# Fifteen instead of thirteen column blocks in the first projections, and their weight loads in program order

## The chip, the cores and the metric

The kernel runs on one core of one Trainium2 chip. A core has a matrix engine (TensorE, PE in the profile), a vector engine (DVE), a scalar engine for activations and casts (ACT), GpSimd (POOL) and a synchronisation engine (SP), whose queue here starts nearly all transfers from memory. Each engine works through its own list of instructions in order and waits on semaphores for the others. The metric is the device time of one execution in microseconds (us); of several executions the median is taken.

## What is computed

One layer of a hybrid decoder, 256 tokens of width 2048, everything in float32:

```
mod = silu(c) @ w_ada + b_ada                       # six rows of 2048: sh1, sc1, gt1, sh2, sc2, gt2
h = rmsnorm(x, g_mix) * (1 + sc1) + sh1
z = h @ w_in
(mq, mk, mv, mo, mi, mf, dq, dk, dv, sq, sk, sv, gm, gd, gs) = split_cols(z, IN_SIZES)
out_m = mlstm(mq, mk, mv, mi, mf, mo)
out_d = differential_attention(dq, dk, dv)
out_s = stick_breaking_attention(sq, sk, sv)
merged = (sigmoid(gm) * (out_m @ w_branch[0])
          + sigmoid(gd) * (out_d @ w_branch[1])
          + sigmoid(gs) * (out_s @ w_branch[2]))    # gs, the third gate: 2048 columns, in four blocks of 512
x = x + gt1 * (merged @ w_out)
h = rmsnorm(x, g_ffn) * (1 + sc2) + sh2
hid = h @ w_up
x = x + gt2 * ((silu(causal_dwconv(hid[:, :5632])) * hid[:, 5632:]) @ w_down)
```

What the change touches is the projection `z = h @ w_in` and, in it, the columns of `gs`.

## The kernel before, in words

**Matrix products in three passes.** Weights and activations are float32. `weights()` (L330) loads 4 k-tiles (4 x 128 rows) of a column block of up to 512 columns, 1 MB, in one transfer on SP's queue (L337) into one of three buffers `raw`; ACT casts two k-tiles at a time into a rounded part `hi` (L342), DVE subtracts to get the rest `lo` (L344), and `gemm()` (L350) sums three products: hi by both parts of the activations, lo by the rounded part. So a block of 512 columns over all 16 k-tiles is 96 matmuls of 512 columns: per k-tile and token half, three of them. There are four buffers each for `hi` and `lo`. Blocks of only 2 k-tiles use a smaller buffer, `raw2`. Results gather in banks of PSUM: three called `gp` and four called `mx` (the function `bank`), which short work uses.

**The start.** `h` is not there at once: its scale and shift come from `silu(c) @ w_ada`, a product that DVE does by multiply-add (`ada_mac`, L217) while 4096 columns of `w_ada` arrive. It is made in pieces of 2 to 4 k-tiles: k-tiles 0 and 1 first, 2 and 3 next (`ada_first`), then 4 to 7, 8 to 11 and 12 to 15 (`ada_quad`, L272). Each finished piece lets `make_h` (L458) produce those k-tiles of `h`. Meanwhile the first projections run on the k-tiles that exist. The list `first` (L508 to L516) holds 13 column blocks: 0 to 3 are sq and sk, 4 and 5 are sv, 6 to 12 are 440 columns wide and hold mi, mf, dq, dk and dv. `visit()` (L560) goes over a range of blocks up to a given k-tile and sets a rate; `partial()` (L521) does one block from the k-tile where it stopped. Between visits the partial sums of a block lie in the destination tile. They are copied out by ACT (L549), copied back into PSUM (L538) before the next visit, or added by DVE (L551); blocks 0 and 1 keep banks of their own.

**Side work.** After each group of 4 k-tiles `tick()` (L209) takes steps from two lists: `ada` (the pieces of w_ada) and `side` (everything else that can lie beside matmuls). `rates` says how many steps a tick takes. When the k-tiles wanted aren't there, `partial` takes steps until they are.

**Order of transfers.** A load in `weights()` carries `issue_after(state["load"].ins)`, that is, it's placed behind the load before it in SP's queue, only the first time (`started`, L335). Later ones may be placed earlier by the scheduler that lays out each engine's list. The steps of `ada` always carry it (L262, L278, L292).

**Behind the first projections.** A last loop (L892 to L895) brings the 13 blocks to k-tile 16; at block 5 it appends `stick()`, stick-breaking attention, to the side list. `stick` goes through four pairs of heads. Each pair works in the tile `ez` in slot 9 (a slot is one of the large tiles, `slot(i, name)`): scores, log terms, sums along the row through `puA` and `puB` (L615 to L620), subtraction (L621, L622), exponential (L623), masks (L626, L627), then the product with sv into `po` (L632, L634), which is split into `osh` and `osl` (L636). Behind the loop the gate blocks 0 and 1 of `gs` go into `mg0` (slot 8), the side list is emptied, `mg1` is allotted in slot 9, where `ez` was, `diff()` is appended (its first step squares dq into `dsq`, L645), and gate blocks 2 and 3 go through a sigmoid on ACT (L851) into `mg1`.

`late_vectors()` (L138) loads small vectors on POOL's queue into `rows2`, a tile in slot 3, where the input x lay until it was transposed at the start.

Of the kernel before, what the change touches and what calls it, by code (L numbers as in the profile page):

```python
# [12 lines left out]
AF = mybir.ActivationFunctionType  # L13
# [4 lines left out]
P = 128  # L18
# [21 lines left out]
def kernel(  # L40
# [97 lines left out]
    def late_vectors():  # L138
        rows = slot(3, "rows2")
        rowsB, rowsC = rows[0:27, 0:P], rows[0:64, P:2 * P]  # L140
        rowsD = rows[0:NF, 2 * P:5 * P].rearrange("k (j p) -> k j p", j=3)
        def ld(*args):
# [11 lines left out]
        ld(bif, b_gate_if.rearrange("o (g h) -> h (o g)", h=MH))  # L154
        lamv = rows[0:1, 640:896].rearrange("o (v d) -> o v d", v=4)
        for i, lv in enumerate((lam_q1, lam_k1, lam_q2, lam_k2)):
# [11 lines left out]

        lp = rows[0:1, 896:1024].rearrange("o (v d) -> o v d", v=2)
        V.tensor_tensor(lp, lamv[:, 0::2, :], lamv[:, 1::2, :], ALU.mult)  # L170
# [21 lines left out]
    ada = deque()  # L192
    state = {"ada": 0.0, "side": 0.0, "split": None, "load": None, "hold": None, "h": 0, "started": False}

# [135 lines left out]
    def weights(rows, nk, n, hold=None):  # L330
        if nk == 2:
            raw = adap.tile([P, 2, 512], F32, tag="ada", name="raw2")
        else:
            raw = rawp.tile([P, 4, 512], F32, tag="raw", name="raw")
        with tc.issue_after(state["load"].ins) if not state["started"] else nullcontext():  # L335
            state["started"] = True
            state["load"] = nc.sync.dma_start(raw[:, :nk, :n], rows.rearrange("(k p) f -> p k f", p=P))  # L337
        his, los = [], []
        for k0 in range(0, nk, 2):
            hi = hip.tile([P, 2, 512], F32R, tag="hi", name="hi")  # L340
            lo = lop.tile([P, 2, 512], F32R, tag="lo", name="lo")
            A.copy(hi[:, :, :n], raw[:, k0:k0 + 2, :n])  # L342
            with tc.issue_after(hold.ins) if hold else nullcontext():
                state["split"] = V.tensor_tensor(lo[:, :, :n], raw[:, k0:k0 + 2, :n], hi[:, :, :n].bitcast(F32),  # L344
                                                 ALU.subtract)
            his.append(hi)
            los.append(lo)
        return his, los
# [166 lines left out]
    for i in range(7):  # L515
        first.append(("T", C_IF + 440 * i, 440, dest_D(i), 1.0))  # L516

    def shaped(src, dst):
        return src.rearrange("p (a b) -> p a b", a=dst.shape[1]) if len(dst.shape) == 3 else src

    def partial(ci, kt0, kt1):  # L521
# [21 lines left out]
        for b in range(2):  # L543
            for cs, d in dest(b):
# [3 lines left out]
                elif put or kt0 == 0:  # L548
                    A.copy(d, shaped(acc[b][:, cs], d))  # L549
                else:  # L550
                    V.scalar_tensor_tensor(d, shaped(acc[b][:, cs], d), scale, d, ALU.mult, ALU.add)  # L551
        tick()

# [3 lines left out]
    ada.extend(ada_quad(k0, quads[:, (i % 2) * 1024:(i % 2 + 1) * 1024]) for i, k0 in enumerate((4, 8, 12)))  # L557
    done = [0] * 13

# [5 lines left out]

    visit(range(0, 9), 2, 0.72)
    visit(range(9, 13), 4, 2.1)
    visit(range(0, 9), 4, 1.1)
    side.append(late_vectors())
    rates["side"] = 0.4  # L570
    visit(range(0, 10), 8, 1.72)
    visit(range(10, 13), 12, 1.36)
    visit(range(0, 7), 12, 1.36)
    drain(ada)
    drain(side)


# [313 lines left out]
    rates["side"] = 2.4  # L891
    for ci in range(13):  # L892
        partial(ci, done[ci], 16)
        if ci == 5:
            side.append(stick())  # L895


    rates["side"] = 2.0
    rates["ada"] = 0.9
    mg.append(slot(8, "mg0"))  # L900
    for ch in range(2):
        gates(C_GS, ch, mg_of(ch))
    drain(side)
# [213 lines left out]
```

## Time and profile before

| what | value |
|---|---|
| median of 3 runs | 1791.58 us (1788.38 to 1792.2) |
| time of the profiled execution | 1787.35 us |
| span of the profiled execution, first to last instruction | 1785.6 us |
| mean granted TensorE clock | 0.999 |
| read from memory, written | 419.68 MB, 2.10 MB |
| mean transfer rate over the span | 237 GB/s |

Times in the views are in microseconds from the first instruction of the profiled execution. Busy time of PE is the sum of stretches in which some matmul is recorded as running; a matmul's record is longer than its share of a steady stream (389 ns for 512 columns), because matmuls are pipelined and overlap. So a short wait hides in the overlap and shows in the distance of the starts rather than as idle time. In the view of windows, a row is a stretch: its length, then busy time (and count) of PE, of PE's weight loads, DVE, ACT and POOL, the granted clock, the busy share of the DMA engines, and GB/s. In a timeline row stand start, length, engine, line, operation, and in brackets how long the engine was idle ahead of it and on what it waited.

### The profile page before, as it was taken

The numbers are of one execution on the slowest core, as the hardware profiler recorded it, in microseconds if no ns is written. First come the engines' busy times: TensorE is split into PE (matmuls) and PEld (weight loads), VectorE is DVE, ScalarE is ACT, GpSimd is POOL, SyncE is SP. The second block draws the span as 40 slices with busy tenths as digits, with TensorE's granted clock in tenths as the row PEclk, the third lists the DMA queues.
The fourth block names the chain that finished last, engine by engine and source line by source line (L and its number), as shares of the span: only waits on it lengthen the run. The fifth ranks groups of instructions, "written<-read, shape, count | busy, mean of one in ns | idle before, by whom it ended". The sixth has DMA issues, their size and how long they took to land.

```text
span 1785.6 us, 23761 instructions
## 1 busy us (share of the span) xinstructions
PE 1762.2 (99%) x9168; PEld 1512.5 (85%) x9168; DVE 1302.4 (73%) x1734; ACT 951.9 (53%) x1338; POOL 16.4 (1%) x44
## 2 busy tenths in 40 slices
PE   7899999999999999999999999999999999999998
PEld 6898999888878887888888888888888888888887
DVE  6887646878888778777996577888875556666654
ACT  6667655666565556544444555555553345555432
POOL 2000000000000000000000000000000000000000
PEclk9999999999999999999999999999999999999999
DMA  9999855776777567778896547777755555555563
GB/s 338 346 330 313 289 179 178 266 244 242 248 238 259 200 216 251 240 261 294 308 323 216 181 166 259 253 251 267 268 204 198 193 189 189 189 189 189 189 214 117
DMA packets 219731, 423.33 MB, mean 237 GB/s; under 512 B 9027, under 2 KB 31675, under 8 KB 219105
## 3 DMA queue, kind: packets, MB, share of 16 engines
q1 hardware_dynamic: 217328, 417.44, 68.8%
q0 software_dynamic: 1008, 2.23, 0.4%
q10 hardware_dynamic: 1280, 2.14, 0.3%
q8 instruction: 72, 1.18, 0.3%
q14 instruction: 43, 0.34, 0.1%
HBM read 419.68 MB, written 2.10 MB: 236 GB/s over the span
## 4 chain that ended last, share of the span: by engine, by line
PE 95%; ACT 2%; DMA 1%; DVE 1%; issue 1%; SPq 0%; ACTq 0%
PE gp L391 55%; PE acch L377 32%; PE kept L396 2%; PE gp L396 2%; DMA raw<-in_w_in_dram 1%; ACT hi L342 1%; PE psc L679 0%; PE pm L240 0%; DMA x<-in_x_dram 0%; DVE quads L224 0%; PE spin L186 0%; ACT x L444 0%; PE pr L321 0%; PE pxt L453 0%; PE ptf L739 0%
## 5 line engine op out<-in xcount | busy, mean ns | idle before, releaser
L344 DVE TENSOR_TENSOR lo<-raw,hi 128x1024 fp32r<-128x1024 f32 (+1 forms) x608 | 724.0, 1208 | 363.4 <-ACT hi L342 327.1
L342 ACT CAST hi<-raw 128x1024 fp32r<-128x1024 f32 (+1 forms) x608 | 617.6, 1039 | 552.4 <-PE gp L391 353.6
L391 PE MATMUL gp<-hi,h 128*128 128x512 f32 (+1 forms) x1600 | 411.4, 387 | 7.0 <-ACT hi L342 5.7
L377 PE MATMUL acch<-h,hi 128*128 128x512 f32 x1664 | 403.3, 392 | 0.2 <-DVE h L1032 0.2
L377 PEld LDWEIGHTS acch<-h,hi 128*128 128x128 f32 x1664 | 303.6, 188 | 58.0 <-DVE h L1032 1.1
L391 PEld LDWEIGHTS gp<-hi,h 128*128 128x128 f32 x1600 | 295.7, 188 | 60.7 <-ACT hi L342 8.8
L391 PE MATMUL gp<-lo,h 128*128 128x512 f32 (+1 forms) x800 | 227.5, 384 | 0.0
L377 PEld LDWEIGHTS acch<-h,lo 128*128 128x128 f32 x1664 | 217.8, 191 | 11.1
L377 PE MATMUL acch<-h,lo 128*128 128x256 f32 x1664 | 221.3, 283 | 0.0
L224 DVE SCALAR_TENSOR_TENSOR acc<-araw,ccol,acc 128x512 f32<-128x512 f32 x240 | 179.3, 748 | 6.0 <-DMA araw<-in_w_ada_dram 4.3
L391 PEld LDWEIGHTS gp<-lo,h 128*128 128x128 f32 x800 | 149.7, 188 | 26.2 <-DVE lo L344 0.8
L391 PE MATMUL gp<-hi,atl 128*128 128x512 f32 x352 | 137.2, 390 | 0.0
L391 PE MATMUL gp<-hi,ath 128*128 128x512 f32 x352 | 136.9, 389 | 0.0
L391 PE MATMUL gp<-lo,ath 128*128 128x512 f32 x352 | 105.9, 390 | 0.0
L391 PEld LDWEIGHTS gp<-hi,atl 128*128 128x128 f32 x352 | 66.1, 188 | 13.7
L391 PEld LDWEIGHTS gp<-hi,ath 128*128 128x128 f32 x352 | 66.1, 188 | 13.7
L391 PEld LDWEIGHTS gp<-lo,ath 128*128 128x128 f32 x352 | 66.1, 188 | 13.6
L224 DVE SCALAR_TENSOR_TENSOR quads<-raw,ccol,quads 128x1024 f32<-128x1024 f32 x45 | 57.7, 1282 | 2.8 <-DMA raw<-in_w_ada_dram 2.2
L391 PE MATMUL gp<-hi,mgl 128*128 128x512 f32 x128 | 50.4, 394 | 0.0
L391 PE MATMUL gp<-hi,mgh 128*128 128x512 f32 x128 | 50.0, 392 | 0.0
L1057 DVE SCALAR_TENSOR_TENSOR y<-gsum,cols,y 128x255 f32<-128x255 f32 (+1 forms) x88 | 41.4, 479 | 3.7 <-ACT y L1055 3.5
L391 PE MATMUL gp<-lo,mgh 128*128 128x512 f32 x128 | 38.3, 391 | 0.0
(365 smaller groups left out, 1601.2 us busy)
## 6 DMA issues: line engine op xcount, KB each, us to landing
raw<-in_w_in_dram SPq DMA_DIRECT2D x98, 1024.0 KB, 5.1
raw<-in_w_up_dram SPq DMA_DIRECT2D x88, 1024.0 KB, 5.1
araw<-in_w_ada_dram SPq DMA_DIRECT2D x128, 512.0 KB, 5.9
raw<-in_w_down_dram SPq DMA_DIRECT2D x44, 1024.0 KB, 5.1
raw<-in_w_ada_dram SPq DMA_DIRECT2D x62, 512.0 KB, 5.9
raw<-in_w_branch_dram SPq DMA_DIRECT2D x24, 1024.0 KB, 5.1
raw<-in_w_in_dram SPq DMA_DIRECT2D x25, 880.0 KB, 5.0
raw<-in_w_out_dram SPq DMA_DIRECT2D x16, 1024.0 KB, 5.0
```

What stands on the lines that cost most here:

```text
L224: state["mac"] = V.scalar_tensor_tensor(acc, raw[:, k, :], ccol[:, kt:kt + 1], acc, ALU.mult, ALU.add)
L342: A.copy(hi[:, :, :n], raw[:, k0:k0 + 2, :n])
L344: state["split"] = V.tensor_tensor(lo[:, :, :n], raw[:, k0:k0 + 2, :n], hi[:, :, :n].bitcast(F32), ALU.subtract)
L377: T.matmul(acc[t][:, 0:m], lhsT=w[k // 2][:, k % 2, sl], rhs=ah(s0 + k)[:, 0:m], start=start, stop=s0 + k == kt1 - 1 and w is (wh if flip ...
L391: T.matmul(o, lhsT=a(s0 + k)[:, sl], rhs=wk[:, :n], **kw)
L396: T.matmul(o, lhsT=wk[:, sl], rhs=a(s0 + k), **kw)
L1057: V.scalar_tensor_tensor(yf[:, sft:S], src[:, 0:S - sft], wc(2 - sft), yf[:, sft:S], ALU.mult, ALU.add)
```

## The change

Three things change together.

Gate blocks 0 and 1 of `gs` become blocks 13 and 14 of `first`. Their partial sums lie in `gsp`, a tile in slot 3, and behind their last part a sigmoid writes `mg0`; the separate loop of two gate blocks behind the first projections goes away, and `mg0` is allotted ahead of the last loop. The last loop takes 13 and 14 first. Since slot 3 is taken, `late_vectors` uses two small tiles of the pool `sidewide`.

Weight loads are kept in program order up to the end of the visits (`inorder`), not only the first.

The visits and rates are others, as the diff shows.

```diff
@@ -136,9 +136,9 @@
     nlam = const.tile([P, 1], F32, name="nlam")
 
     def late_vectors():
-        rows = slot(3, "rows2")
+        rows, rows3 = sidewide("rows2"), sidewide("rows3")
         rowsB, rowsC = rows[0:27, 0:P], rows[0:64, P:2 * P]
-        rowsD = rows[0:NF, 2 * P:5 * P].rearrange("k (j p) -> k j p", j=3)
+        rowsD = rows3[0:NF, 0:3 * P].rearrange("k (j p) -> k j p", j=3)
         def ld(*args):
             with tc.issue_after(state["load"].ins):
                 nc.gpsimd.dma_start(*args)
@@ -152,7 +152,7 @@
         ld(rowsC, w_mconv[0].rearrange("j (k p) -> (j k) p", p=P))
         ld(rowsD, w_ffconv[0].rearrange("j (k p) -> k j p", p=P))
         ld(bif, b_gate_if.rearrange("o (g h) -> h (o g)", h=MH))
-        lamv = rows[0:1, 640:896].rearrange("o (v d) -> o v d", v=4)
+        lamv = rows[0:1, 2 * P:4 * P].rearrange("o (v d) -> o v d", v=4)
         for i, lv in enumerate((lam_q1, lam_k1, lam_q2, lam_k2)):
             ld(lamv[:, i, :], lv)
         yield
@@ -166,7 +166,7 @@
         V.tensor_scalar(gsub_c, gsub_c, 1.0 - LAM_INIT, None, ALU.mult)
         V.tensor_scalar(gdq_c, gdq_c, 64.0 ** -0.5, None, ALU.mult)
 
-        lp = rows[0:1, 896:1024].rearrange("o (v d) -> o v d", v=2)
+        lp = rows3[0:1, 3 * P:4 * P].rearrange("o (v d) -> o v d", v=2)
         V.tensor_tensor(lp, lamv[:, 0::2, :], lamv[:, 1::2, :], ALU.mult)
         ls = const.tile([1, 2], F32, name="ls")
         V.tensor_reduce(ls, lp, AX.X, ALU.add)
@@ -190,7 +190,7 @@
 
     side = deque()
     ada = deque()
-    state = {"ada": 0.0, "side": 0.0, "split": None, "load": None, "hold": None, "h": 0, "started": False}
+    state = {"ada": 0.0, "side": 0.0, "split": None, "load": None, "hold": None, "h": 0, "inorder": True}
 
     def pump(queue, n):
         done = 0
@@ -332,8 +332,7 @@
             raw = adap.tile([P, 2, 512], F32, tag="ada", name="raw2")
         else:
             raw = rawp.tile([P, 4, 512], F32, tag="raw", name="raw")
-        with tc.issue_after(state["load"].ins) if not state["started"] else nullcontext():
-            state["started"] = True
+        with tc.issue_after(state["load"].ins) if state["inorder"] else nullcontext():
             state["load"] = nc.sync.dma_start(raw[:, :nk, :n], rows.rearrange("(k p) f -> p k f", p=P))
         his, los = [], []
         for k0 in range(0, nk, 2):
@@ -514,6 +513,9 @@
         first.append(("T", C_SV + ch * 512, 512, dest_T(sv, ch), 1.0))
     for i in range(7):
         first.append(("T", C_IF + 440 * i, 440, dest_D(i), 1.0))
+    gsp = slot(3, "gsp")
+    for ch in range(2):
+        first.append(("T", C_GS + ch * 512, 512, dest_T(gsp, ch), 1.0))
 
     def shaped(src, dst):
         return src.rearrange("p (a b) -> p a b", a=dst.shape[1]) if len(dst.shape) == 3 else src
@@ -549,13 +551,15 @@
                     A.copy(d, shaped(acc[b][:, cs], d))
                 else:
                     V.scalar_tensor_tensor(d, shaped(acc[b][:, cs], d), scale, d, ALU.mult, ALU.add)
+                    if ci > 12:
+                        A.activation(mg_of(ci - 13)[b], d, AF.Sigmoid)
         tick()
 
     kept = {}
     quads = slot(4, "quads")
     ada.append(ada_first(2))
     ada.extend(ada_quad(k0, quads[:, (i % 2) * 1024:(i % 2 + 1) * 1024]) for i, k0 in enumerate((4, 8, 12)))
-    done = [0] * 13
+    done = [0] * 15
 
     def visit(cis, kt1, rate):
         rates["ada"] = rate
@@ -563,16 +567,17 @@
             partial(ci, done[ci], kt1)
             done[ci] = kt1
 
-    visit(range(0, 9), 2, 0.72)
-    visit(range(9, 13), 4, 2.1)
-    visit(range(0, 9), 4, 1.1)
+    visit(range(0, 9), 2, 0.6)
+    visit(range(9, 15), 4, 1.4)
+    visit(range(0, 9), 4, 0.85)
     side.append(late_vectors())
     rates["side"] = 0.4
-    visit(range(0, 10), 8, 1.72)
-    visit(range(10, 13), 12, 1.36)
-    visit(range(0, 7), 12, 1.36)
+    visit([13, 14, *range(0, 10)], 8, 1.45)
+    visit([*range(10, 13)], 8, 1.45)
+    visit([13, 14, *range(0, 6)], 12, 1.45)
     drain(ada)
     drain(side)
+    state["inorder"] = False
 
 
     def stick():
@@ -889,17 +894,15 @@
 
     ada.append(ada_rest())
     rates["side"] = 2.4
-    for ci in range(13):
+    mg.append(slot(8, "mg0"))
+    for ci in (13, 14, *range(13)):
         partial(ci, done[ci], 16)
         if ci == 5:
             side.append(stick())
-
-
-    rates["side"] = 2.0
+            rates["ada"], rates["side"] = 0.5, 2.8
+
+
     rates["ada"] = 0.9
-    mg.append(slot(8, "mg0"))
-    for ch in range(2):
-        gates(C_GS, ch, mg_of(ch))
     drain(side)
     mg.append(slot(9, "mg1"))
     side.append(diff())
```

No matmul is added or taken away. On SP's list, this is what stands where the first visit ends. `raw_586<-in_w_in` is the load of block 8 for k-tiles 0 and 1; a load of 4x440 is one of blocks 9 to 12 for k-tiles 0 to 3; `raw_793`, `raw_827` and `raw_866` are loads of blocks 0, 1 and 2 for k-tiles 2 and 3, which belong to the third visit; 2x512 of w_ada are the two halves of a step of `ada_quad`. Before:

```order
L337 DMA raw_586<-in_w_in_dram 128x2x440
L337 DMA raw<-in_w_in_dram 128x4x440
L337 DMA raw_793<-in_w_in_dram 128x2x512
L337 DMA raw_827<-in_w_in_dram 128x2x512
L279 DMA raw_651<-in_w_ada_dram 128x2x512 x2
L337 DMA raw<-in_w_in_dram 128x4x440
L337 DMA raw_866<-in_w_in_dram 128x2x512
L279 DMA raw_698<-in_w_ada_dram 128x2x512 x2
L337 DMA raw<-in_w_in_dram 128x4x440
L279 DMA raw_743<-in_w_ada_dram 128x2x512 x2
L337 DMA raw<-in_w_in_dram 128x4x440
```

With the change, from the same load (here `raw_567`) on; 4x512 are blocks 13 and 14, and `raw_869` and `raw_900` are blocks 0 and 1 of the third visit:

```order
L336 DMA raw_567<-in_w_in_dram 128x2x440
L279 DMA raw_607<-in_w_ada_dram 128x2x512 x2
L336 DMA raw<-in_w_in_dram 128x4x440 x2
L279 DMA raw_694<-in_w_ada_dram 128x2x512 x2
L336 DMA raw<-in_w_in_dram 128x4x440
L279 DMA raw_739<-in_w_ada_dram 128x2x512 x2
L336 DMA raw<-in_w_in_dram 128x4x440
L336 DMA raw<-in_w_in_dram 128x4x512
L279 DMA raw_822<-in_w_ada_dram 128x2x512 x2
L336 DMA raw<-in_w_in_dram 128x4x512
L336 DMA raw_869<-in_w_in_dram 128x2x512
L336 DMA raw_900<-in_w_in_dram 128x2x512
```

The three loads of the third visit stood among those of the second; now the third visit's loads stand behind all six of the second, and steps of w_ada lie between.

On PE's list, the end of `stick`'s fourth pair of heads, from the sums `puA` to the product `po`; `gp_3531` and `gp_3532` are the banks of gate block 2. Before:

```order
L616 MATMUL puA_3242<-loA_3235,tri_97 128x512
L619 MATMUL puA_3242<-hlB_3236,ones_r_92 128x2x128
L620 MATMUL puA_3242<-hlB_3236,ones_r_92 128x2x128
L391 MATMUL gp_3531<-hi_3585,h1_138 128x512 x4
L391 MATMUL gp_3531<-lo_3586,h1_138 128x512 x2
L391 MATMUL gp_3532<-hi_3585,h1_138 128x512 x4
L391 MATMUL gp_3532<-lo_3586,h1_138 128x512 x2
L230 MATMUL pm_3613<-ident_85,acc_3229 128x128 x4
...
L391 MATMUL gp_3531<-hi_3642,h1_139 128x512 x2
L632 MATMUL po_3293<-ez_2709,sv_303 128x256
L391 MATMUL gp_3531<-hi_3642,h1_139 128x512
L634 MATMUL po_3293<-ez_2709,sv_303 128x128
```

With the change, the same place; `gp_3559` and `gp_3560`, which hold gate block 2, are full by then, and `gp_3768` and `gp_3769` are the banks of gate block 3:

```order
L390 MATMUL gp_3768<-hi_3832,h1_138 128x512 x4
L623 MATMUL puB_3387<-hlB_3342,tri_97 128x256
L621 MATMUL puA_3386<-loA_3341,tri_97 128x512
L624 MATMUL puA_3386<-hlB_3342,ones_r_92 128x2x128
L625 MATMUL puA_3386<-hlB_3342,ones_r_92 128x2x128
L390 MATMUL gp_3768<-lo_3833,h1_138 128x512 x2
L637 MATMUL po_3399<-ez_2883,sv_303 128x256
L639 MATMUL po_3399<-ez_2883,sv_303 128x128
L637 MATMUL po_3399<-ez_2883,sv_303 128x256
L639 MATMUL po_3399<-ez_2883,sv_303 128x128
L390 MATMUL gp_3769<-hi_3772,h1_138 128x512 x4
L390 MATMUL gp_3769<-lo_3773,h1_138 128x512 x2
```

Before, 26 matmuls of gate block 2 and a transpose in four parts stood between `puA` and `po`; now two matmuls do, and the first of `gp_3769` stands behind `po`. There are three `gp` banks: `gp_3769` takes the one in which `gp_3559` lay.

On ACT's list, the same place: the exponential of the fourth pair, the split of `po` (`osh`), the first step of `diff` (`dsq`) and the sigmoid of gate block 2 (`mg1`). Before:

```order
L623 ACT_TABLE_LOAD
L623 ACTIVATE ez_2709<-ez_2709 128x768
L342 CAST hi_3698<-raw_3692 128x1024
L342 CAST hi_3744<-raw_3742 128x1024
L418 CAST osh_2707<-po_3293 128x512
L645 ACTIVATE dsq_3571<-dq_304 128x2048
L342 CAST hi_3748<-raw_3742 128x1024
L851 ACT_TABLE_LOAD
L851 ACTIVATE mg1_3530<-gp_3531 128x512
```

With the change:

```order
L341 CAST hi_3832<-raw_3826 128x1024
L628 ACT_TABLE_LOAD
L628 ACTIVATE ez_2883<-ez_2883 128x768
L417 CAST osh_2881<-po_3399 128x512
L650 ACTIVATE dsq_3599<-dq_304 128x2048
L856 ACT_TABLE_LOAD
L856 ACTIVATE mg1_3558<-gp_3559 128x512
L856 ACTIVATE mg1_3558<-gp_3560 128x512
```

The two casts behind the exponential and the one behind `dsq` are gone from here, and the sigmoid still stands behind the exponential, `osh` and `dsq`. The bank of `gp_3559` comes free when this sigmoid has read it.

## The prediction

> **What bounds the kernel now.** First the busy shares and the chain of work that ended last:
>
> ```profile
> PE 1762.2 (99%) x9168; PEld 1512.5 (85%) x9168; DVE 1302.4 (73%) x1734; ACT 951.9 (53%) x1338; POOL 16.4 (1%) x44
> PE 95%; ACT 2%; DMA 1%; DVE 1%; issue 1%; SPq 0%; ACTq 0%
> 1319.67 129.21 PE gp L391 x570
> ```
>
> PE is busy for 1762.2 of 1785.6 us, and the chain lies on it for 95%. The third row is one unbroken stretch of that chain: 570 matmuls of 512 columns in 129.21 us, 0.227 us each. That is the step of a steady stream, and since the change has the same matmuls, only time in which PE waits can be gained or lost. Second view, windows of the first 500 us (length; busy time and count of PE, weight loads, DVE, ACT, POOL; clock; DMA share; GB/s):
>
> ```profile
> 26.00:45.00 19.00, 18.01 (x122) 16.02 (x120) 16.24 (x24) 8.22 (x14) 3.48 (x7) 1.00 1.08 350
> 45.00:60.00 15.00, 13.43 (x72) 12.10 (x73) 12.29 (x19) 10.41 (x22) 0.00 (x0) 1.00 1.02 369
> 60.00:75.00 15.00, 11.98 (x61) 10.52 (x60) 10.39 (x10) 6.92 (x12) 0.00 (x0) 1.00 0.90 300
> 75.00:90.00 15.00, 15.00 (x111) 14.73 (x111) 13.78 (x13) 11.10 (x18) 0.00 (x0) 1.00 1.02 369
> 90.00:110.00 20.00, 20.00 (x123) 18.07 (x122) 19.10 (x30) 18.19 (x32) 0.00 (x0) 1.00 0.90 318
> 110.00:135.00 25.00, 24.74 (x185) 23.23 (x184) 19.52 (x18) 11.29 (x16) 0.00 (x0) 1.00 0.96 330
> 135.00:160.00 25.00, 23.16 (x116) 19.84 (x115) 20.67 (x26) 20.68 (x43) 0.00 (x0) 1.00 0.91 307
> 160.00:225.00 65.00, 64.96 (x404) 61.13 (x403) 43.65 (x44) 41.20 (x67) 0.00 (x0) 1.00 0.86 296
> 300.00:400.00 100.00, 100.00 (x477) 85.97 (x476) 81.17 (x113) 64.22 (x71) 0.00 (x0) 1.00 0.73 246
> 400.00:500.00 100.00, 100.00 (x496) 80.79 (x495) 87.54 (x146) 59.20 (x115) 0.00 (x0) 1.00 0.72 247
> ```
>
> Length less PE's busy time, summed over the first eight rows, is 0.99 + 1.57 + 3.02 + 0 + 0 + 0.26 + 1.84 + 0.04 = 7.7 us of idle PE. Behind 300 us there is none. So the early stretch, to 225 us, is what there is to gain, and everything later can only be lost. The 7.7 is a low reading, because a matmul's record outlasts its step and hides the start of each wait. I therefore also took every start of PE in this stretch (the counts of the eight rows make 1194) less the start before it and less the steady step of its shape (0.227 for 512 columns, 0.200 for 440, 0.120 for 256); the first and the last of these rows are
>
> ```profile
> 26.65 0.74 PE L396 MATMUL kept<-h,hi 128*128 128x256 f32 x4 [0.41 <-ACT h L465]
> ...
> 225.01 0.39 PE L391 MATMUL gp<-lo,h 128*128 128x512 f32 x1
> ```
>
> and the sum is 13.2 us. I take 13.2 as all that the early stretch can give. What it waits on:
>
> ```profile
> PE gp L391 <- ACT hi L342: 5.7, 5, 1.6
> PE gp L391 <- ACT gp L538: 0.9, 1, 0.9
> ...
> 60.15 0.53 ACT L549 COPY dk<-gp 128x440 f32<-128x440 f32 x1 [2.37 <-PE gp L391]
> 61.15 0.53 ACT L549 COPY dk<-gp 128x440 f32<-128x440 f32 x1 [0.47 <-PE gp L391]
> 61.57 1.75 ACT L342 CAST hi<-raw 128x880 fp32r<-128x880 f32 x2
> 62.55 0.47 PE L391 MATMUL gp<-hi,h 128*128 128x440 f32 x1 [1.44 <-ACT hi L342]
> ```
>
> Nearly all of it is a wait for the cast of the next weights, in five waits of at most 1.6 us. The timeline shows two causes behind one name. ACT works in order, so at 60 to 63 us the cast at 61.57 stands behind the copies of the block before; and where ACT itself was waiting, it was for a load, in a stretch where the DMA share is 0.90 to 1.08.
>
> **Early: two more blocks and program order.** Blocks 13 and 14 bring 4 k-tiles x 6 matmuls x 2 blocks x 0.227 = 10.9 us of PE work into the second visit, at 75 us and before, work that PE does on k-tiles of h that it has, while w_ada for the next k-tiles arrives. They bring 2 x 1 MB of loads. At the 340 GB/s that the first five rows average by their lengths, 2.1 MB are 6.2 us. So PE gets 10.9 us of cover and the transfers only 6.2 us of work: about 4.7 us of transfer time comes free for w_ada. Program order adds to it: three loads of the third visit, 0.52 MB each, stood ahead of those of the second; 1.57 MB are 4.6 us by which loads that PE waits for at 45 to 70 us can come sooner. Against it stands what order cannot mend: the casts queued behind copies, such as that of 61.57. The new blocks bring more copies of that kind (12 COPY out, 8 back, and 4 additions on DVE). ACT is busy 10.41 of 15 us and DVE 12.29 of 15 in the row from 45, so they are not full, but each copy pair of 2 x 0.53 can stand ahead of a cast. Bounds for the gain: 0 if only ACT's order and the three buffers count, 13.2 if all waits go. Following the loads by hand through the new order at 340 GB/s, h for k-tiles 4 to 7 comes some 5 us sooner against PE's work than now. I take **-5**, nearer to the waits shown for the load-bound rows (45 to 75: 1.57 + 3.02 = 4.6) than to either end.
>
> **Start: POOL.**
>
> ```profile
> 22.85 0.51 POOL L144 DMA_DIRECT2D rows<-in_g_ffn_dram  x1 [19.02 <-PE pxt L453]
> 8.81 4.74 PE L186 MATMUL spin<-ones_r 128*128 128x512 f32 x14
> ```
>
> POOL's small loads waited 19.02 us for the tile that x had held. Their new tiles are free, so they can go from 4 us on, among x and the first w_ada. They are small; between 0 and the 0.5 us of one such row I take **+0.3**.
>
> **Late: the end of stick-breaking.** Here the order of instructions shows a wait that was not there. The rows of before with which I price it:
>
> ```profile
> 294.55 0.69 DVE L621 TENSOR_TENSOR ez<-ez,puA 128x512 f32<-128x512 f32 x1
> 298.41 0.42 DVE L627 TENSOR_TENSOR ez<-ez,mstrict 128x256 f32<-128x256 f32 x1
> ...
> 382.80 0.29 PE L620 MATMUL puA<-hlB,ones_r 128*128 128x256 f32 x1
> 383.14 1.28 ACT L623 ACT_TABLE_LOAD   x1
> 383.19 0.68 DVE L621 TENSOR_TENSOR ez<-ez,puA 128x512 f32<-128x512 f32 x1
> 384.43 0.85 ACT L623 ACTIVATE ez<-ez 128x768 f32<-128x768 f32 x1
> 385.66 0.42 DVE L627 TENSOR_TENSOR ez<-ez,mstrict 128x256 f32<-128x256 f32 x1
> 390.65 0.38 PE L634 MATMUL po<-ez,sv 128*128 128x128 f32 x2
> 391.07 0.59 ACT L418 CAST osh<-po 128x512 fp32r<-128x512 f32 x1 [1.35 <-PE po L634]
> 391.55 1.92 ACT L645 ACTIVATE dsq<-dq 128x2048 f32<-128x2048 f32 x1
> 395.91 1.28 ACT L851 ACT_TABLE_LOAD   x1 [1.51 <-issue]
> 397.20 0.60 ACT L851 ACTIVATE mg<-gp 128x512 f32<-128x512 f32 x1
> ```
>
> From the end of `puA` (383.1) to the end of the masks (386.08) went 2.9 us, and PE did 26 matmuls meanwhile. In the new order two matmuls stand there, 2 x 0.227 = 0.45, then `po`. So PE waits 2.9 - 0.45 = 2.45 us. Behind `po` PE's next instruction is the first matmul of `gp_3769`, and its bank is freed only by the sigmoid that reads `gp_3559`. That sigmoid writes `mg1` into slot 9, where `ez` is until `po` has read it, so it cannot go before `po`, and in ACT's list it stands behind `osh` and `dsq` as before. From the end of `po`: 391.07 - 391.03 = 0.04, `osh` to the start of `dsq` 0.48, `dsq` 1.92, table 1.28, sigmoid 0.60, and some 0.1 to PE: 4.4 us in which PE has nothing else in its list. Everything on PE stands behind it. Nothing covers it: it costs **2.45 + 4.4 = 6.9 us**. Low bound 4.4, if PE comes late to `po` for another reason and the first wait vanishes. For the upper bound, the first pair took 294.55 to 298.83, 4.3 us (to the end of the second row), where casts and splits lay between; with 4.3 in place of 2.9 and a price of the clock of 1.6 (below) it is 9.9.
>
> The row of 383.14 weighs a rule on tables: the exponential starts 0.01 us after its 1.28 us table load. The Trainium skill, "ScalarE: Activation LUTs", section "What ACT_TABLE_LOAD costs", gives a drain of about 1.38 us besides the 1.28, 2.66 for a switch. By it the last wait would be 1.38 longer and the sum 1795.2. The trace bears out the 1.28 and shows no drain at 383.14: the cast ahead of it ended 0.02 us before, so I leave it out.
>
> **The sum.** The profiled execution took 1787.35 (its span 1785.6 and 1.75 around it): 1787.35 - 5 + 0.3 + 6.9 = 1789.55. The median shown is 1791.58, 4.23 above that execution, so on its scale the time is 1789.55 + 4.23 = **1793.8**. The rest of the edits cost nothing that I can name: 15 more ACT instructions of 0.5 us lie in stretches where ACT has 4.6 of 15 us free, and all behind 600 us is unchanged.
>
> **Rivals.**
>
> *Faster: the early waits go altogether.* Transfers are what the stretch from 26 to 75 waits for (DMA share around 1), and the loads in order end that; -13.2 + 0.3 + 6.9 gives 1785.6. Against it are the copies ahead of the casts, and the 1.84 us of waits in the row from 135, behind the last visits' loads, which the change leaves. To be faster by over 0.2% (about 3.6 us, what a measurement can tell from no change) the early gain must pass 10.8. 0.15.
>
> *Slower: the early stretch does not gain, and the change does not do what it says.* The queue is full from 26 to 60 us (350 and 369 GB/s), so the same bytes and 2.1 MB more have to pass before h is complete, whatever their order; and in the row from 60 to 75, where PE idles most, the rate is 300: there it is ACT's order and three buffers that bind. Then the gain is 0, the late wait stays, 0 + 0.3 + 6.9 gives 1798.8. It decides for slower as soon as the early gain is under 3.6. 0.25.
>
> *Slower: the pause costs clock.* The granted clock is 1.00 in every row above, and the longest wait in the early stretch is 1.6 us. The 4.4 us at `gp_3769` would be much longer. If the clock falls there, the nearest price is PE's start: 14 matmuls took 4.74 us at 8.81 instead of 14 x 0.227 = 3.18, 1.6 more; 1793.8 + 1.6 = 1795.4. 0.10. The Trainium skill, "TensorE: Matmul & The Clock Gate", section "Why this matters for your kernels", says so: no PE-idle gaps over about 3 us between bursts, or the clock goes back to half. No run here shows a gap that long.
>
> **How the numbers follow.** The forecast, 1793.8, has 0.50. Its own spread, gains of 3 to 7.5 early, gives 1791.3 to 1795.8. The cases of slower hold 0.25, half of 0.10, and of the forecast the part with a gain under 3.6, some 0.07: 0.37. Faster 0.15, within 0.2% the remaining 0.48. The range takes in both ends, the faster rival at 1785.6 and the slower one at 1798.8 with something for the clock: 1785 to 1800.
>
> **What would show it.** Early: idle PE from 26 to 225 us down from 7.7 to about 3 to 5, with fewer waits for `hi`. Late: two waits of PE near the end of `stick`, one at `po` for DVE's masks of 2 to 3 us, one at the next `gp` for ACT of about 4.4, with PE's busy time in that window below its length for the first time behind 300 us. I am wrong if that second wait is absent or under 2 us, if the early idle time doesn't fall, or if the granted clock after the wait is below 1.

## The result, and the profile after

| | median | lowest to highest | runs |
|---|---|---|---|
| before | 1789.53 us | 1786.35 to 1792.77 | 14 |
| with the change | 1794.3 us | 1791.88 to 1796.72 | 14 |

The ratio is 1.0023, with a 95% interval of 1.0016 to 1.0031: the change makes the kernel slower by about 4 us (the two medians lie 4.8 apart). The profiled execution, the shortest of the 14, has a span of 1790.2 us where before had 1785.6, 4.6 more. The page of the changed kernel, its busy shares and the dearest group of matmuls:

```profile
PE 1763.7 (99%) x9168; PEld 1515.1 (85%) x9168; DVE 1305.5 (73%) x1738; ACT 965.8 (54%) x1353; POOL 16.3 (1%) x44
L390 PE MATMUL gp<-hi,h 128*128 128x512 f32 (+1 forms) x1600 | 411.0, 386 | 8.1 <-ACT mg L856 4.4
```

PE has the same 9168 matmuls. What ends most of the idle time ahead of `gp` is now the sigmoid that writes `mg`, 4.4 us, where it was the cast `hi`. The early stretch as one window, of before and then of the changed kernel:

```profile
26.00:225.00 199.00, 191.28 (x1183) 175.66 (x1182) 155.65 (x177) 128.02 (x219) 3.48 (x7) 1.00 0.93 320
```

```profile
26.00:225.00 199.00, 195.31 (x1161) 178.32 (x1161) 156.15 (x174) 135.23 (x224) 0.00 (x0) 0.99 0.93 322
```

Idle PE went from 199 - 191.28 = 7.7 to 199 - 195.31 = 3.7 us. Summed over the distances of starts, as in the prediction, the time above the steady step went from 13.2 to 8.2 (with other steps for the small shapes both are 1 to 1.5 higher, and the fall 5.3). The profiles of the runs below that leave the early stretch alone bear the fall out: idle PE in this window is 7.7 to 9.4 us in the three with the stretch of before (before, e6, e12) and 3.3 to 4.6 in the eight with that of the changed kernel (it, e1 to e3, e7 to e10). Their spread, up to 1.7 us with the same instructions, is also how far one profile can be trusted here.

The first matmul on `h` starts later with the change, at 27.73 us where the prediction shows 26.65 for before. On ACT, the third cast of weights stands ahead of the rows that make `h`; it waited for its load and began at 26.12, where before had it at 25.05:

```profile
26.12 1.05 ACT L341 CAST hi<-raw 128x1024 fp32r<-128x1024 f32 x1 [0.35 <-DMA raw<-in_w_in_dram]
27.08 1.09 ACT L464 ACTIVATE h<-xnT,b,a 128x256 fp32r<-128x256 f32 x2
27.73 1.01 PE L395 MATMUL kept<-h,hi 128*128 128x256 f32 x3 [0.83 <-ACT h L464]
```

PE's largest waits from 26 to 225 us, with the change:

```profile
PE gp L390 <- DVE h L418: 1.4, 1, 1.4
PE kept L395 <- ACT h L464: 0.8, 1, 0.8
PE gp L390 <- ACT h L417: 0.5, 1, 0.5
PE gp L390 <- ACT hi L341: 0.4, 2, 0.2
```

The waits for the cast of the next weights, 5.7 us before, are 0.4. What is left is mostly a wait for h itself. Later, where the view of before names no wait of PE from 225 to 600 us, there are now these (and one of 0.2 at `ptf`):

```profile
PE gp L390 <- ACT mg L856: 4.4, 1, 4.4
PE po L637 <- DVE ez L631: 1.8, 1, 1.8
PE gp L390 <- ACT mv L928: 1.2, 1, 1.2
```

The first two lie together. The timeline of the changed kernel there (PE and ACT, and DVE's masks):

```profile
397.33 0.63 PE L390 MATMUL gp<-lo,h 128*128 128x512 f32 x2
398.33 0.84 ACT L628 ACTIVATE ez<-ez 128x768 f32<-128x768 f32 x1 [3.94 <-DVE ez L626]
399.55 0.42 DVE L632 TENSOR_TENSOR ez<-ez,mstrict 128x256 f32<-128x256 f32 x1
399.78 0.67 PE L637 MATMUL po<-ez,sv 128*128 128x256 f32 x2 [1.82 <-DVE ez L631]
...
401.36 0.58 ACT L417 CAST osh<-po 128x512 fp32r<-128x512 f32 x1 [2.19 <-PE po L639]
401.84 1.91 ACT L650 ACTIVATE dsq<-dq 128x2048 f32<-128x2048 f32 x1
...
403.77 1.28 ACT L856 ACT_TABLE_LOAD   x1
...
405.07 1.09 ACT L856 ACTIVATE mg<-gp 128x512 f32<-128x512 f32 x2
405.72 1.79 PE L390 MATMUL gp<-hi,h 128*128 128x512 f32 x4 [4.39 <-ACT mg L856]
```

Four matmuls of 512 columns took 1.79 us behind the gap, against 1.08 and 1.09 for the groups of four at 394.08 and 395.82. The windows around it show why, in the column of the clock:

```profile
396.00:406.00 10.00, 3.79 (x19) 2.86 (x19) 5.92 (x8) 5.45 (x6) 0.00 (x0) 1.00 0.44 157
406.00:411.00 5.00, 5.00 (x16) 3.90 (x16) 1.87 (x3) 3.61 (x4) 0.00 (x0) 0.66 0.00 0
411.00:420.00 9.00, 9.00 (x42) 7.42 (x41) 9.00 (x9) 7.31 (x8) 0.00 (x0) 1.00 0.58 195
```

In the 5 us behind the wait the granted clock was 0.66. Some eight starts there lie 0.43 apart instead of 0.227, so this cost 8 x 0.2 = 1.6 us.

### The profile page after: what moved, and what is told of

It reads as the page before. It is cut to its first block, busy times and chain, and to the rows that moved or that the text cites. A ratio compares the mean times of both kernels' runs of the same rounds, so it can differ in the third digit from the quotient of the medians.

```text
span 1790.2 us, 23763 instructions
## 1 busy us (share of the span) xinstructions
PE 1763.7 (99%) x9168; PEld 1515.1 (85%) x9168; DVE 1305.5 (73%) x1738; ACT 965.8 (54%) x1353; POOL 16.3 (1%) x44
## 4 chain that ended last, share of the span: by engine, by line
PE 95%; ACT 2%; DVE 2%; DMA 1%; issue 1%; SPq 0%; DVEq 0%; ACTq 0%
PE gp L390 53%; PE acch L376 32%; PE kept L395 3%; PE gp L395 3%; DMA raw<-in_w_ada_dram 1%; PE psc L684 0%; DMA raw<-in_w_in_dram 0%; ACT hi L341 0%; DVE lo L343 0%; DVE acc L224 0%; PE pm L240 0%; SPq L263 0%; PE pr L321 0%; PE pmg L882 0%; PE pdt L669 0%
## 5 line engine op out<-in xcount | busy, mean ns | idle before, releaser
L390 PE MATMUL gp<-hi,h 128*128 128x512 f32 (+1 forms) x1600 | 411.0, 386 | 8.1 <-ACT mg L856 4.4
L390 PEld LDWEIGHTS gp<-hi,h 128*128 128x128 f32 x1600 | 297.0, 188 | 60.7 <-ACT mg L856 4.6
L390 PE MATMUL gp<-lo,h 128*128 128x512 f32 (+1 forms) x800 | 230.5, 384 | 0.0
L390 PEld LDWEIGHTS gp<-lo,h 128*128 128x128 f32 x800 | 149.7, 188 | 25.8 <-issue 1.0
L390 PE MATMUL gp<-hi,atl 128*128 128x512 f32 x352 | 136.9, 389 | 0.0
L390 PE MATMUL gp<-hi,ath 128*128 128x512 f32 x352 | 136.8, 389 | 0.0
L390 PE MATMUL gp<-lo,ath 128*128 128x512 f32 x352 | 105.8, 389 | 0.0
L390 PEld LDWEIGHTS gp<-hi,atl 128*128 128x128 f32 x352 | 66.1, 188 | 13.8
L390 PEld LDWEIGHTS gp<-hi,ath 128*128 128x128 f32 x352 | 66.0, 188 | 13.7
L390 PEld LDWEIGHTS gp<-lo,ath 128*128 128x128 f32 x352 | 66.1, 188 | 13.7
L390 PE MATMUL gp<-hi,mgl 128*128 128x512 f32 x128 | 50.3, 393 | 0.0
L390 PE MATMUL gp<-hi,mgh 128*128 128x512 f32 x128 | 50.0, 392 | 0.0
L395 PE MATMUL kept<-h,hi 128*128 128x256 f32 x256 | 39.2, 289 | 0.8 <-ACT h L464 0.8
```

The costliest lines, as they stand in the source:

```text
L390: T.matmul(o, lhsT=a(s0 + k)[:, sl], rhs=wk[:, :n], **kw)
L395: T.matmul(o, lhsT=wk[:, sl], rhs=a(s0 + k), **kw)
```

## The experiments

All ratios are to the kernel before, on the same chip in the same series.

**e1_wide: gate block 2 no longer writes into the slot of ez.**

```diff
-    for ch in range(2, 4):
-        gates(C_GS, ch, mg_of(ch))
+    sg2 = [wide("sg"), wide("sg")]
+    gates(C_GS, 2, sg2)
+    gates(C_GS, 3, mg_of(3))
...
-                sg = mg_of(ch)
+                sg = sg2 if ch == 2 else mg_of(ch)
...
-                V.tensor_tensor(sg[tt], accb[tt], sg[tt], ALU.mult)
+                V.tensor_tensor(sg[tt] if order else d, accb[tt], sg[tt], ALU.mult)
```

> The changed kernel, but gate block 2 goes through its sigmoid into two small tiles of the pool wide instead of into mg1, the slot in which stick-breaking's ez lies; the product with the branch writes mg1 later. Nothing else is changed. Theory (the shared slot makes the late wait): PE's waits for ez (1.8 us) and for the sigmoid (4.4 us) go, and with them the clock of 0.66 in the 5 us behind them (1.6 us), so about 7.8 us less than the changed kernel: ratio to before 1.0023 - 0.0044 = 0.998, some 1786.5 us. Rival (the fourth pair of heads is late by itself, and freeing the bank only moves the wait to po or to the branch product that needs its output): ratio 1.001 to 1.0025, with a wait of 3 us or more for po, osl or dsq in its place.

Measured: 1.0026 (1.0015 to 1.0037). The late wait went, and nothing was won. PE's waits from 225 to 600 us in this run:

```profile
PE ptf L744 <- DVE od L732: 6.7, 1, 6.7
PE gp L390 <- ACT mv L929: 1.2, 1, 1.2
```

The rival held, at another place than it named. With the bank free, the order of PE put more matmuls ahead of the fourth pair's `po`, which now ended at 409.2 us instead of 401.3. `diff` begins behind it, so `diff` began later as well, and its last step `ptf` was waited for at 556.8 to 563.5 us with no matmul left to cover it. The clock fell there too, which the window shows:

```profile
556.00:568.00 12.00, 4.63 (x23) 3.71 (x21) 6.78 (x9) 6.25 (x11) 0.12 (x1) 0.72 0.18 63
```

So the shared slot is where the wait came up, and not what it is made of.

**e2_late_diff: diff appended one gate block later.**

```diff
-    side.append(diff())
     rates["side"] = 2.9
-    for ch in range(2, 4):
-        gates(C_GS, ch, mg_of(ch))
+    gates(C_GS, 2, mg_of(2))
+    side.append(diff())
+    gates(C_GS, 3, mg_of(3))
```

> The changed kernel, but diff() is appended behind gate block 2 instead of ahead of it, so that its 1.9 us square does not stand between the split of po and the sigmoid on ACT. Theory (the wait is the length of ACT's list between po and the sigmoid): the wait for the sigmoid falls from 4.4 to about 2.5 us. If the clock falls only after a gap of some length, and 2.5 is below it, 1.6 us go as well: 3.5 us less than the changed kernel, ratio 1.0003; if it falls all the same, 1.9 us less, ratio 1.0012. Rival (the wait is for something else than ACT's list): the wait stays above 4 us, ratio 1.0023. The later start of diff may lengthen the wait of 1.2 us for mv near 566 us; that is read from the trace separately.

Measured: 1.0004 (0.9995 to 1.0014). The waits, and the window behind the shorter one:

```profile
PE gp L390 <- ACT mg L856: 2.6, 1, 2.6
PE po L637 <- DVE ez L631: 1.8, 1, 1.8
```

```profile
405.00:410.00 5.00, 5.00 (x24) 4.14 (x23) 4.96 (x4) 5.00 (x6) 0.00 (x0) 1.00 0.01 3
```

Taking the 1.9 us square out of ACT's list between `po` and the sigmoid took 1.8 us out of the wait, and at 2.6 us the clock stayed at 1.00 in this trace. The wait came as expected. Whether the clock held in every execution the time doesn't say: the interval holds both times that were expected, 1.0003 and 1.0012, and the trace is of one of the shortest (1787.73 us; the twelve took 1787.68 to 1793.62).

**e3_warm: PE kept at work through the wait.** Here 18 matmuls are added whose result is not used.

```diff
-                T.matmul(po[:, j * S + P:(j + 1) * S], lhsT=sv[:, MW + hp:MW + hp + P], rhs=zB[:, j], start=False,
-                         stop=True, skip_group_check=True)
+                last = T.matmul(po[:, j * S + P:(j + 1) * S], lhsT=sv[:, MW + hp:MW + hp + P], rhs=zB[:, j], start=False,
+                         stop=True, skip_group_check=True)
+            if h == HEADS - 2:
+                with tc.issue_after(last.ins):
+                    spin(18, bank("warm"))
```

> The changed kernel with 18 idle matmuls of 512 columns (4.1 us) added on PE behind the fourth pair's po, into a bank that nobody reads, so that PE works through the wait for the sigmoid. Theory (of the late cost, 1.5 to 1.6 us are the clock that falls in the gap): the gap between po and the next block's first matmul stays 4.4 us long but is filled, the granted clock in the 5 us behind it is 1.0 instead of 0.66, and the time is 1.5 us less than the changed kernel, ratio 1.0015. Rival (the slow matmuls behind the gap come from something else, such as their weights): they stay at a step of 0.43 us, ratio 1.0023 or above.

Measured: 1.0009 (0.9999 to 1.0018).

```profile
400.02 4.34 PE L186 MATMUL warm<-ones_r 128*128 128x512 f32 x18
404.67 1.20 PE L390 MATMUL gp<-hi,h 128*128 128x512 f32 x4 [0.31 <-ACT mg L859]
```

The next block began 4.65 us behind the start of the idle matmuls, so the wait itself is about as long as before, and its four first matmuls took 1.20 instead of 1.79 us. The clock was 1.00 here. The interval holds the expected 1.0015 and not the rival's 1.0023; the trace, of the shortest of eleven executions, shows the slow starts behind the wait gone.

**e4_no_order and e5_order_only: the order of the loads.** e4 is the changed kernel with only the first load held in order:

```diff
+            state["inorder"] = False
             state["load"] = nc.sync.dma_start(raw[:, :nk, :n], rows.rearrange("(k p) f -> p k f", p=P))
```

> The changed kernel, but only the first weight load is held in program order, as before the change; later ones may be placed earlier again. Three loads of the third visit then stand among those of the second again. Theory as in the prediction (of the early gain of 5 us about half is the order of the loads, half the two blocks that join): PE's idle time from 26 to 225 us rises by 2 to 3 us from 3.7, ratio 1.0035. Rival (the gain is all from the two blocks and the pace): no change early, ratio 1.0023. The other rival (the gain is all from the order): idle time back at 7.7 or more, ratio 1.005.

Measured: 1.0024 (1.0015 to 1.0034), the same as with the order. PE's idle time from 26 to 225 us didn't rise (3.3 us against 3.7), but the kind of wait changed, from waits for h to waits for the cast:

```profile
PE gp L391 <- ACT hi L342: 2.6, 3, 2.0
```

e5 is the kernel before with the order and nothing else:

```diff
-        with tc.issue_after(state["load"].ins) if not state["started"] else nullcontext():
-            state["started"] = True
+        with tc.issue_after(state["load"].ins) if state["inorder"] else nullcontext():
...
     drain(ada)
     drain(side)
+    state["inorder"] = False
```

> The kernel before, with the program order of weight loads up to the end of the visits and nothing else of the change. The run without the order (e4) came out like the changed kernel, so the theory now is that order is worth little: PE's idle time from 26 to 225 us stays between 6.5 and 8 us (7.7 before), ratio 0.9995 to 1.0005. Rival, that of the prediction (order is worth half of the early 5 us): idle time 5 us or less, ratio 0.9986.

Measured: 1.0011 (1.0003 to 1.002). PE's waits for the cast from 26 to 225 us in e5, in the two orientations of the blocks:

```profile
PE gp L390 <- ACT hi L341: 3.6, 5, 1.5
PE gp L395 <- ACT hi L341: 2.8, 4, 1.6
```

The order took none of the waits away, 6.4 us here against 5.9 before (5.7 at L391 and 0.2 at L396). It moved some of them, from the blocks of L390 to those that are computed the other way round (L395), whose loads the order had set back. With the change's pace it decides which wait it is, and makes no difference to the time that can be measured; by itself it costs a little.

**e11_old_pace: the rates of before in the six visits.**

```diff
-    visit(range(0, 9), 2, 0.6)
-    visit(range(9, 15), 4, 1.4)
-    visit(range(0, 9), 4, 0.85)
+    visit(range(0, 9), 2, 0.72)
+    visit(range(9, 15), 4, 2.1)
+    visit(range(0, 9), 4, 1.1)
...
-    visit([13, 14, *range(0, 10)], 8, 1.45)
-    visit([*range(10, 13)], 8, 1.45)
-    visit([13, 14, *range(0, 6)], 12, 1.45)
+    visit([13, 14, *range(0, 10)], 8, 1.72)
+    visit([*range(10, 13)], 8, 1.72)
+    visit([13, 14, *range(0, 6)], 12, 1.36)
```

> The changed kernel with the rates of ada steps of before in the six visits (0.72, 2.1, 1.1, 1.72, 1.72, 1.36); blocks, ranges and order as changed. Theory (the two blocks give the early gain, by covering w_ada's transfer; the rates matter little): PE's time above the steady step from 26 to 225 us stays at 7 to 9 us (8.2 with the change, 13.2 before), ratio 1.0018 to 1.0028. Rival (the pace gives it): 11 us or more, ratio 1.0038 or above.

Measured: 1.0058 (1.0045 to 1.0071). The rival held. The early stretch and its waits in this run:

```profile
26.00:225.00 199.00, 190.25 (x1082) 171.37 (x1082) 155.32 (x178) 132.05 (x226) 0.00 (x0) 0.97 0.91 320
```

```profile
PE gp L390 <- ACT hi L341: 4.8, 4, 1.8
PE gp L390 <- ACT gp L540: 1.5, 2, 1.0
PE kept L395 <- ACT hi L341: 1.3, 1, 1.3
```

PE is idle for 8.75 us, as much as in the profiles of before, and the waits for `hi` are back. By the distances of starts 18.1 us are lost, 10 more than with the changed pace. That is too much for this edit: the trace is of an execution of 1802.4 us, the longest of five, with a clock of 0.97 over the stretch, and the other four took 1796.6 to 1797.4. By the ratios (1.0058 against 1.0023) the old pace costs some 6 us, which is about the early gain. So with the two blocks and the old pace that gain is not there.

**e6_before_late_stick: the kernel before, with its side work begun later.**

```diff
-        if ci == 5:
+        if ci == 8:
             side.append(stick())
```

> The kernel before, with stick-breaking appended to the side list behind block 8 instead of block 5 of the last loop, and nothing of the change. On PE's list the fourth pair's puA and po then stand half a microsecond of matmuls apart and ahead of the last gp bank, as in the changed kernel. Theory (the late cost is stick-breaking that ends later against PE's work, because blocks 13 and 14 were taken from beneath it, and not the blocks or their loads): the same two waits, about 1.8 us for ez and 4.4 for the sigmoid, and a clock of about 0.66 behind them, 7.8 us in all, ratio 1.0044; the early stretch is as before. Rival (the waits come from the changed kernel's other edits, its pace or its loads): no wait over 1 us there, ratio 1.000.

Measured: 1.0075 (1.0062 to 1.0088).

```profile
PE gp L391 <- ACT mg L851: 4.4, 1, 4.4
PE po L632 <- DVE ez L626: 2.2, 1, 2.2
PE gp L391 <- ACT mv L925: 0.7, 1, 0.7
```

One line makes the kernel before show the same three waits, without a block, a load or a rate of the change. It cost 13 us rather than the 8 expected: by the distances of starts 10.4 us lie between 390 and 425 us, 0.9 about `mv`, and the early stretch of this run lost 2 more than that of before. The last isn't this edit: PE's idle time there is 9.4 us here and 8.9 in e12, which has the early instructions of before as well (7.7). Between 390 and 425 us the clock took more than in the changed kernel:

```profile
405.00:420.00 15.00, 8.40 (x26) 6.68 (x27) 6.72 (x8) 9.53 (x10) 0.00 (x0) 0.66 0.13 52
```

A clock of 0.66 over 15 us is half the clock for 0.34 x 15 / 0.5 = 10.2 us, where the changed kernel had it for 0.34 x 5 / 0.5 = 3.4.

**e7_stick_first and e8_first_wide: blocks 13 and 14 behind block 5 in the last loop.** e7 is this edit on the changed kernel, e8 the same on e1:

```diff
-    for ci in (13, 14, *range(13)):
+    for ci in (*range(6), 13, 14, *range(6, 13)):
```

> The changed kernel, but the last loop takes blocks 0 to 5, then 13 and 14, then 6 to 12, so that stick-breaking begins 11 us of PE work earlier. mg1 still lies where ez was. On PE's list 37 matmuls stand between the fourth pair's puA and po, and two behind po ahead of the bank that the sigmoid frees. Theory: the wait of 1.8 us at po goes, the wait for the sigmoid is 4.4 - 0.45 = 3.9 us and the clock falls behind it: 2.3 us less than the changed kernel, ratio 1.0010. Rival (with more work ahead of it the fourth pair is early enough and the sigmoid is done in time): no late wait, ratio 0.998.

> The changed kernel with both: the last loop in the order of e7, and gate block 2's sigmoid into two tiles of the pool wide, as in e1. In e1 the late wait went, but 6.7 us came back at ptf, because diff began later against PE's work. Here diff's last product stands 7 us of PE work ahead of ptf, where in e1 it stood 0.2 ahead. Theory (stick and diff are one chain of side work that has to be done by ptf, and an earlier start gives it room): no wait over 0.5 us for po, mg1 or ptf; only the 1.2 us for mv stays; 7.8 us less than the changed kernel, ratio 0.9979, and faster than before. Rival (the chain is bound by DVE and ACT whatever its start): 4 us or more at ptf, ratio 1.000 or above.

Measured: e7 1.0038 (1.0024 to 1.0052), e8 1.0005 (0.9996 to 1.0014). PE's largest waits from 225 to 600 us of e7, and two windows of it:

```profile
PE gp L390 <- ACT mg L856: 3.9, 1, 3.9
PE ptf L744 <- DVE od L732: 2.1, 2, 1.7
PE gp L390 <- ACT mv L928: 1.0, 1, 1.0
```

```profile
405.00:410.00 5.00, 4.72 (x11) 3.79 (x12) 3.02 (x3) 3.56 (x5) 0.00 (x0) 0.50 0.00 0
570.00:575.00 5.00, 3.96 (x11) 3.07 (x11) 3.14 (x7) 3.97 (x9) 0.12 (x1) 0.53 0.00 0
```

In e7 the wait for `po` went and the one for the sigmoid is 3.9, as expected. But 2.1 us came up at `ptf`, and the clock fell twice. So neither theory nor rival gave its time. The trace is of an execution of 1798.2 us with a mean clock of 0.995; two of the five took 1793.6 with 0.999, so the two falls are not in every execution. In e8 the late waits are gone, but the same two at `ptf` (2.1) and `mv` (1.2) stay, where under 0.5 was expected at `ptf`. Less than half of what the theory promised came.

**e9_room and e10_room_two_tiles: room for the tail.** e9 is e8, e10 is e1, both with this (and slot 3 made as large as slot 2, so that `mv` fits):

```diff
...
-    drain(side)
-    mv = slots.tile([P, NT, MH, MDH + 1], F32, tag="s2", name="mv")
+    mv = slots.tile([P, NT, MH, MDH + 1], F32, tag="s3", name="mv")
...
-    mqT, mkT = slot(3, "mqT"), slot(4, "mkT")
+    drain(side)
+    mqT, mkT = slot(2, "mqT")[:, 0:2048], slot(4, "mkT")
```

> e8 with room for the tail of diff: mv lies in slot 3 instead of slot 2, where diff's od is, the side list is emptied behind the two blocks of mv instead of ahead of them, and mqT takes slot 2. On PE's list 16 us of matmuls then stand between diff's last product and ptf, instead of 7. Theory (what e8 lost against the early gain is the chain's tail, 2.1 us at ptf and 1.2 at mv): both waits go, 3.5 us less than e8: ratio to before 1.0005 - 0.0020 = 0.9985. Rival (the tail is bound by DVE and comes back in the next stage, at mq or at the branch): 2 us or more of PE's waits there, ratio 1.0000 or above.

> The changed kernel with its own order of the last loop, gate block 2's sigmoid in two tiles of wide as in e1, and mv in slot 3 with the list emptied behind it as in e9. On PE's list 14 us of matmuls stand between diff's last product and ptf, where in e1 it was 0.2. Theory: e1's 6.7 us at ptf and 1.2 at mv go with their clock, and nothing takes their place; the early gain of 5 us is left: ratio 0.9977 to 0.9985. Rival as in e9: 1.0000 or above.

Measured: e9 0.9989 (0.998 to 0.9998), e10 0.9983 (0.9974 to 0.9993), medians of 1785.85 and 1784.54 us against 1787.7 for before. The windows of e10 where after had its late waits:

```profile
390.00:410.00 20.00, 20.00 (x93) 16.59 (x92) 15.36 (x20) 11.18 (x11) 0.00 (x0) 1.00 0.70 245
540.00:590.00 50.00, 50.00 (x263) 42.40 (x262) 37.46 (x52) 28.29 (x39) 0.00 (x0) 1.00 0.59 205
```

PE is busy throughout both, and from 225 to 700 us the view of waits names none for PE in e10. So with room for the chain the late waits are gone, and the changed kernel is faster than before: by 3.2 us in e10, with an interval of 1.3 to 4.6, of the 5 that it gains early.

**e12_before_room: the same room in the kernel before.** The edit is that of e9, on the kernel before.

> The kernel before with mv in slot 3 and the list emptied behind it, as in e9, and nothing else. It has no wait at ptf or mv, so there is nothing to gain: ratio 0.9995 to 1.0005. If it is faster by as much as e9 and e10 are, then what they gain does not come from the change's early stretch.

Measured: 1.0006 (0.9997 to 1.0015). The room is worth nothing where the chain isn't late; what e10 gains comes from the change together with the room.

## Why the prediction came out as it did

The time forecast was 1793.8 and 1794.3 was measured. That they lie so close is luck: the forecast was for a difference of +2.2 us, and it is 4 to 5; but it stood on a median of three executions, 1791.58, and 14 of the same kernel have 1789.53, 2.05 lower. The two misses cancel. Step by step:

- **Early, -5: the size was about right, the reason was not.** The sum of start distances fell by 5.0 (13.2 to 8.2). I gave it to two things, cover by the two blocks and loads in order. The order is worth nothing in time (e4, e5). And I did not cost the pace at all: with the old rates the whole gain is gone (e11). The step "h for k-tiles 4 to 7 comes some 5 us sooner" failed as well. In the changed kernel h comes later, the first of k-tiles 4 to 7 at 112.2 instead of 100.5 us and of 8 to 11 at 186.4 instead of 149.8, and 11.7 us is no sooner even against the 10.9 us of work that the blocks add by then. With the slower pace and the order the waits for `hi` go from 5.7 to 0.4 us, and without the order to 2.6 (e4). My reading is that the slower pace leaves the queue and DVE to the weights, and that the two blocks give PE work to do until the later h arrives. That both are needed is shown for the pace only; the new pace without the two blocks was not tried.
- **Start, +0.3: too small.** The first matmul on h starts at 27.73 instead of 26.65 us, behind the same 87 matmuls: 1.1 us. All ten profiles with the changed start have it at 27.66 to 27.95, the four with that of before (before, e5, e6, e12) at 26.53 to 26.80. Within 26 us the distances of starts give 0.2 to 0.6 of it, by the steps taken for the small shapes; the rest lies in the window from 26 us on, so that the early gain without it is 5.5 to 5.9 rather than 5.0. Neither the order (e4: 27.71) nor the pace (e11: 27.78) makes it. A load of weights that lands later is what the rows show; that POOL's small loads, which go from 3.76 us on instead of 22.85, hold it up is likely, but no run tests them alone.
- **Late, 6.9: the place and both waits were right.** 1.8 at `po` where 2.45 was worked out, 4.4 at the sigmoid where 4.4 was. (The chain taken as 2.9 is 386.08 - 383.09 = 3.0 by its rows, which makes the first wait 2.5.) The 0.6 too much at `po` is mostly the table load, which I had counted in the chain from `puA` to the masks; in the changed kernel ACT had loaded the table at 393.11 and the exponential went 0.03 us behind DVE. e2 shows that the second wait is ACT's list, piece by piece.
- **The clock, a rival at 0.10, happened:** 1.6 us at a clock of 0.66, the price given. By the prediction's own signs, which name a clock below 1 behind the wait, it was wrong here: the term stood at nothing in the sum. e3 took it away by keeping PE at work. The Trainium skill, "TensorE: Matmul & The Clock Gate", section "Why this matters for your kernels", says that no idle gap of PE between bursts of matmuls may pass about 3 us. The traces agree as far as single waits go: behind 4.39 us the clock fell, behind 2.58 (e2) it did not.
- **Not foreseen: the 1.2 us at `mv`,** the tail of `diff`, which begins 10 us later than before. It lies at 565 us, where the sum has no term; I had not looked at what waits for the end of `diff`.

With these, -5.0 + 0.2 + (1.8 + 4.4) + 1.6 + 1.2 = +4.2 (with -5.9 and +1.1 in place of the first two it is the same), and what is left to the 4.6 between the spans is spread over small differences.

On tables the measurement decides against the Trainium skill's drain of about 1.38 us ("ScalarE: Activation LUTs", "What ACT_TABLE_LOAD costs"): the load at 403.77 follows `dsq`'s end (403.75) by 0.02, and the sigmoid follows the load by 0.02.

What I had read as a wait with its own cause is one place of a larger thing. `stick` and `diff` are one chain of side work, and it has to be done by `ptf`. The change took two gate blocks, 2 x 96 x 0.227 = 43.6 us of matmuls, from beneath that chain and put them ahead of it. In exchange its visits leave k-tiles 8 to 11 of blocks 6 and 10 to 12, 4 x 24 x 0.200 = 19.2 us, to the last loop, where they run beneath the chain. That is 24.4 us more ahead of it, less the early gain; it began at 289.8 instead of 270.1 us, 19.7 later. e6 makes the same waits by a later start alone, e1 shows that the wait goes on to the next place where the chain is needed, and e9 and e10 that it is gone when the chain has room. The other rates of side work in the last loop (2.8 instead of 2.4) were not tried by themselves. Why 7 us of matmuls ahead of `ptf` did not cover it in e7 and e8 is read from the timeline only: from the end of `diff`'s last copy to `ptf` went 8.1 us in e8 (550.6 to 558.7), with DVE's other work in between, and 6.3 in e1 (557.2 to 563.5), where PE stood still.

## What to carry to other kernels

Matmuls that are moved to fill one gap may be what covered something else: before moving them, find which chain of other engines ran beneath them, where its end is needed, and how much cover is left ahead of that place. A wait that vanishes when a buffer is freed, without any time won, was only the first place at which a late chain was needed; follow the chain to its last consumer and give it room there. And rates or paces that ride along with a change are to be costed like any other edit, since here the gain was gone without them.

## What the runs showed of the hardware

The granted clock doesn't follow from the length of a gap alone. It fell behind single waits of 3.9 (e7) and 4.39 us (after) and held at 2.58 (e2). But e7 and e8 have the same three short waits near `ptf` and `mv` (1.7 the longest), and the clock was 0.53 behind them in e7 and stayed up in e8:

```profile
540.00:570.00 30.00, 26.73 (x129) 21.79 (x128) 23.04 (x30) 16.74 (x24) 0.12 (x1) 1.00 0.54 183
```

So waits that add up to some 3.2 us within some 6 us may or may not cost the clock. Falls also differ in length. With 0.50, which the row of e7 shows, as the clock in a fall, it is half the clock for 3.4 us in the changed kernel and 10.2 in e6, by the sums above, and for 0.28 x 12 / 0.5 = 6.7 us at the 6.7 us wait of e1. The first window behind the start, 26 to 45 us, shows the same: a clock of 0.91 in the changed kernel's profile and 1.00 in those of e2 and e3, whose instructions there are the same. About 1 us of what these two traces gain is therefore not their edit's. It is not chance alone either: eight of the ten profiles with the changed start show 0.82 to 0.91 there, and the four with the start of before 1.00. Why, no run shows.
